# Two value projections in one pass over x, with x's first columns loaded ahead

## The chip, the core and the metric

The kernel runs on one core of a Trainium2 chip. A core has engines that work side by side, each through its own queue of instructions in order: TensorE (PE in the profile, with PEld for loading the stationary operand), VectorE (DVE), ScalarE (ACT), GpSimd (POOL) and SyncE (SP), which here only issues transfers. An instruction waits for semaphores that other engines or transfers raise, and everything behind it on its engine waits too. ScalarE can also issue transfers. The time is device microseconds of one execution, the median over several; lower is better.

## The reference, cut to what matters

The kernel is an encoder trunk of two layers over 256 tokens of width 1024. Each layer begins with an RMSNorm and one input projection, whose columns feed pooling, queries, keys, values and gates:

```python
def _token_mixer(xn, w_in, ...):
    u, q, k, v, g_pool, g_attn = jnp.split(xn @ w_in, SPLITS, axis=-1)
    ...
def reference(x, w_in, ..., norm1, ...):
    h = x
    for layer in range(DEPTH):
        h = h + _token_mixer(_rmsnorm(h, norm1[layer]), w_in[layer], ...)
        h = h + _conv_ffn(_rmsnorm(h, norm2[layer]), w_up[layer], ...)
    return _rmsnorm(h, norm_f)
```

The values v have 3 x 512 columns, one set of 512 for each head group. The change concerns the first two sets (g = 0 and g = 1) of layer 0, with which the kernel begins. Since RMSNorm multiplies row t of x by one number r(t) and column k by a gain, v = r(t) * sum over k of x(t,k) * (gain(k) * w(k,c)): the kernel starts on plain x with weights scaled by the gains, and multiplies by r(t) when it evicts the sums.

## The kernel before

Every operand of a product is split into two parts, a high part h (a cast to the fp32r type) and a low part l (the rest), and a product of 128 channels is three matmuls of 128x512: high by high, low by high, high by low ("hh", "lh", "hl"). The class Weights holds the plan of all weight loads and splits: rows adds a load of w rows, use puts its pieces in line, load and load_by issue its transfers (load_by in parts, on SyncE), open_next makes a piece's split: ScalarE writes the high part (with the gain as scale, line 195; without, line 187), VectorE the low part (lines 196 and 188). The tiles are called raw (as loaded, three buffers), wh and wl (split, five buffers), or take an idle tile of another stage (m2, ybig, at2, k1).

x stands as h, 128 partitions by two tokens t by 1024 columns. The two "halves" t = 0, 1 of the 256 tokens are the rows of the sums. To be the stationary operand, x is turned: turn_x transposes 128-column blocks on TensorE into a PSUM tile xt_ps (line 706), ScalarE casts it to xuh, VectorE subtracts to xul (lines 709, 710).

begin (line 328) issues the first transfers: the gains on ScalarE's queue, then on SyncE x's columns 0 to 511 of both tokens between the first four weight quarters of 256 KB, then columns 512 to 1023. It warms TensorE with products of ones (line 363) and turns the gains into gcol. begin_values_of_x (line 688) is written out by hand, its order kept as it is: it sums the set g = 0 over the eight 128-channel chunks k (line 753), with squares of x on ScalarE and VectorE and the plain turned x (f0, f1) added up from its two parts by VectorE (whole, line 736). Then first_values (line 808), whose order a scheduler sets, makes r_ps (the row factors turned, line 816), multiplies f by gains and row factors and splits it into x2 (lines 820 to 826), the normalised x of all later products, and sums the set g = 1 on the kept xuh and xul in a second pass (line 838). keep_values (line 853) evicts the sums.

Behind this stage TensorE transposes parameters (prm_ps, line 378) and begins the projections of u from x2 (by_rows, rows_ps, line 635). Between them stand three products f_ps of the bias tables (build_bias, line 411), which need rr: VectorE makes it (lines 397, 398) from a small table, rb, loaded after prm_ps.

Of the kernel before, what the change touches and what calls it, by code (L numbers as in the profile page):

```python
# [10 lines left out]
F32 = mybir.dt.float32  # L11
# [5 lines left out]
P = 128  # L17
# [69 lines left out]
class Weights:  # L87
# [42 lines left out]
    def load_by(self, n):  # L130

        src, shape, tag = self.loads[self.n_loaded]
        t = self.pool.tile([P, *shape], F32, tag="raw", bufs=self.RAW, name=f"raw{self.n_loaded}")
# [32 lines left out]
    def open_next(self):  # L166
# [24 lines left out]
        def scaled(j):  # L191
            k = (i * shape[0] + j) % KD
# [25 lines left out]
def encoder(ctx, tc, x, w_in, w_pool, pool_scale, w_a, w_b, w_o, norm1, norm2, w_up, conv_w,  # L218
# [29 lines left out]
    for l in range(DEPTH):  # L248
        for g in range(2):
            c0 = C_V + g * 512  # L250
            slots = (("m2", 0, 2), ("m2", 1, 2), ("ybig",), ("at2",)) if g == 0 else ()
            for j in range(l > 0 and g == 0, 2):
                tag = "k1" if l == 0 and g == 1 and j == 0 else None
                W.use(rows(w_in[l], j * 512, 4, c0, 512, tag), slots[2 * j : 2 * j + 2])
        if l == 0:
            W.n_scaled = len(W.pieces)

# [70 lines left out]
    def begin():  # L328
# [4 lines left out]
        first, second = W.load_by(4), W.load_by(2)  # L333

        def part_of_x(t, n):
            nc.sync.dma_start(out=h[:, t, HALVES[n]], in_=xv[:, t, HALVES[n]])
# [12 lines left out]
        nc.vector.memset(ones, 1.0)  # L349
        make_identity(nc, ident)  # L350
# [6 lines left out]
        warm(ps, ones, WARM[1])  # L357
        return lambda n: warm(ps, ones, n)
# [329 lines left out]
    def begin_values_of_x():  # L688


        more = begin()
# [9 lines left out]
        def turn_x(t, c0, n=4):  # L701

            ks = slice(c0, c0 + n)
            pt = mmp.tile([P, n, P], F32, tag="mm", name="xt_ps")
            for k in range(n):
                nc.tensor.transpose(pt[:, k, :], h[:, t, (c0 + k) * P : (c0 + k + 1) * P], ident)

            def keep():
                nc.scalar.copy(out=xuh[:, ks, t, :], in_=pt)
                nc.vector.tensor_sub(out=xul[:, ks, t, :], in0=pt, in1=xuh[:, ks, t, :].bitcast(F32))  # L710

            return keep

        def square(t, n):
            cc = HALVES[n]
            junk = sm.tile([P, 512], F32, tag="s", name="junk")
            if n == 0:
                nc.scalar.activation(
                    junk, h[:, t, cc], AF.Square, scale=D**-0.5, accum_out=ss[t][:, n : n + 1]
                )  # L720
            else:
                nc.vector.scalar_tensor_tensor(
                    out=junk, in0=h[:, t, cc], scalar=1.0 / D, in1=h[:, t, cc],
                    op0=ALU.mult, op1=ALU.mult, accum_out=ss[t][:, n : n + 1],
                )
# [6 lines left out]
        def whole(n, tag):  # L732

            ks = slice(4 * n, 4 * n + 4)
            f = big.tile([P, 4, 2, P], F32, tag=tag, name="xu")
            nc.vector.tensor_add(out=f, in0=xuh[:, ks].bitcast(F32), in1=xul[:, ks].bitcast(F32))
            return f

        ps = [v_tile() for _ in range(2)]
        chunks, pieces = {}, []  # L740

        def split(k):
            if k % 2 == 0:
                pieces.append(W.n_split)
                chunks[k], chunks[k + 1] = W.open_next()
            return chunks[k]

        def product(t, k, kind):
            wh, wl = W.split[pieces[k // 2]]
            a, w = {"hh": (xuh, wh), "lh": (xul, wh), "hl": (xuh, wl)}[kind]  # L750
            first = k == 0 and kind == "hh"
            last = k == KD - 1 and kind == ("lh" if t else "hl")
            return nc.tensor.matmul(ps[t], a[:, k, t, :], w[:, k % 2, :], start=first, stop=last)  # L753

        def both(k):

            hi, lo = split(k)
            hi()
            return lo()

        def products(*steps):
            for t, k, kinds in steps:
                for kind in kinds:
                    last = product(t, k, kind)
            return last

        keep = turn_x(0, 0, 2), turn_x(0, 2, 2)
        keep[0]()
        both(0)
        keep += (turn_x(1, 0),)  # L770
        keep[1]()
        products((0, 0, ("hh", "lh")))
        keep[2]()
        products((0, 0, ("hl",)))
        both(1)
        products((1, 0, ("hh", "hl", "lh")), *((t, 1, ("hh", "lh", "hl")) for t in range(2)))
        both(2)
        products(*((t, 2, ("hh", "lh", "hl")) for t in range(2)))
        keep = turn_x(0, 4)
        both(3)  # L780
        square(0, 0)
        square(1, 0)
        square(0, 1)
        f0 = whole(0, "q0")
        keep()
        products((0, 3, ("hh", "lh", "hl")))
        keep = turn_x(1, 4)
        both(4)
# [667 lines left out]
```

## Time and profile before

| | us |
|---|---|
| median of 3 runs | 859.83 (858.93 to 860.11) |
| profiled execution | 858.9 |
| its span | 857.1 |
| PE busy in it | 849.9 |

The span is what the profile shows between the first and the last instruction. A line of a timeline gives start and length in us, the engine, the line of the kernel, the operation, "out<-in", the shapes, how many equal ones stand together, and in brackets the idle time ahead of it with what ended it. Durations of matmuls overlap, since they are pipelined: the distance of two starts says more than a length. The windows view gives, for a stretch, the busy time of each engine (PE, PEld, DVE, ACT, POOL, each with the number of instructions), the granted clock, the busy share of the transfer engines, and GB/s.

### The profile page before, as it was taken

The page shows a single profiled execution, that of the slowest core. Times are in us where ns is not written, and L with a number is a line of the kernel's source. Part 1 is how long each engine was busy: PE and PEld are TensorE (multiplying, and loading weights), DVE is VectorE, ACT ScalarE, POOL GpSimd, SP SyncE. Part 2 cuts the span into 40 slices and gives each one's busy share as a digit, 9 for nine tenths or more (in the row PEclk, how much of TensorE's full clock was granted, in tenths as well). Part 3 has the DMA queues.
Part 4 walks back from the last instruction along what each step waited for, and adds up shares of the span by engine and source line. Part 5 has one row for each costly group of instructions (what it writes and reads, how often), then busy time and mean ns, then how long its engine had stood idle before and what let it go on. Part 6 is the DMA issues. An engine that isn't in the chain of part 4 may idle for free.

```text
span 857.1 us, 11247 instructions
## 1 busy us (share of the span) xinstructions
PE 849.9 (99%) x4036; PEld 713.1 (83%) x4036; DVE 648.9 (76%) x914; ACT 476.6 (56%) x691; POOL 20.6 (2%) x53
## 2 busy tenths in 40 slices
PE   9999999999999999999999999999999999999997
PEld 7888888888888888888888889888888888888886
DVE  7967988566757798899556598886567657998874
ACT  7645565444635576767444446654445436766762
POOL 2110000000010000000000000000000000000001
PEclk9999999999999999999999999999999999999999
DMA  9687674764846777777526766747658266777751
GB/s 334 224 251 249 200 255 160 222 229 131 307 152 225 231 243 238 252 246 259 197 99 211 230 227 207 233 152 248 203 199 285 102 216 208 243 241 243 242 195 50
DMA packets 99260, 185.02 MB, mean 216 GB/s; under 512 B 9518, under 2 KB 26110, under 8 KB 99204
## 3 DMA queue, kind: packets, MB, share of 16 engines
q1 hardware_dynamic: 98692, 182.96, 64.3%
q0 software_dynamic: 496, 1.33, 0.6%
q8 instruction: 32, 0.52, 0.2%
q14 instruction: 24, 0.20, 0.1%
q10 hardware_dynamic: 16, 0.00, 0.0%
HBM read 160.12 MB, written 1.07 MB: 188 GB/s over the span
## 4 chain that ended last, share of the span: by engine, by line
PE 99%; ACT 0%; POOLq 0%; DVE 0%; issue 0%; POOL 0%; ACTq 0%
PE rows_ps L635 61%; PE res_ps L551 6%; PE res_ps L549 6%; PE res_ps L550 6%; PE v_ps L635 5%; PE proj_ps L521 3%; PE proj_ps L523 2%; PE v_ps L753 1%; PE v_ps L838 1%; PE s_ps L1020 1%; PE o_ps L1095 1%; PE s_ps L1015 1%; PE o_ps L1091 1%; PE xt_ps L482 1%; PE pool_ps L515 0%; PE pool_ps L514 0%
## 5 line engine op out<-in xcount | busy, mean ns | idle before, releaser
L188 DVE TENSOR_TENSOR wl<-raw,wh 128x1024 fp32r<-128x1024 f32 x278 | 336.8, 1217 | 148.5 <-ACT wh L187 144.7
L635 PE MATMUL rows_ps<-wh,x 128*128 128x512 f32 x1344 | 419.9, 390 | 0.0
L187 ACT CAST wh<-raw 128x1024 fp32r<-128x1024 f32 x278 | 289.4, 1049 | 215.9 <-PE rows_ps L635 129.2
L635 PEld LDWEIGHTS rows_ps<-wh,x 128*128 128x128 f32 x1344 | 252.3, 188 | 51.9
L635 PE MATMUL rows_ps<-wl,x 128*128 128x512 f32 x672 | 261.4, 389 | 0.0
L635 PEld LDWEIGHTS rows_ps<-wl,x 128*128 128x128 f32 x672 | 126.2, 188 | 25.9
L549 PE MATMUL res_ps<-wh,actq 128*128 128x512 f32 (+1 forms) x152 | 57.5, 378 | 0.0
L550 PE MATMUL res_ps<-wl,actq 128*128 128x512 f32 (+1 forms) x152 | 57.4, 378 | 0.0
L551 PE MATMUL res_ps<-wh,actk 128*128 128x512 f32 (+1 forms) x152 | 57.4, 378 | 0.0
L635 PE MATMUL rows_ps<-wh,po 128*128 128x512 f32 x128 | 41.2, 393 | 0.0
L550 PEld LDWEIGHTS res_ps<-wl,actq 128*128 128x128 f32 x152 | 28.6, 188 | 5.4
L549 PEld LDWEIGHTS res_ps<-wh,actq 128*128 128x128 f32 x152 | 28.6, 188 | 5.4
L551 PEld LDWEIGHTS res_ps<-wh,actk 128*128 128x128 f32 x152 | 28.6, 188 | 5.3
L521 PE MATMUL proj_ps<-x,wh 128*128 128x512 f32 x128 | 32.2, 393 | 0.0
L670 DVE STREAM_TRANSPOSE up_rows<-rows_ps 128x512 f32<-128x512 f32 x40 | 26.2, 692 | 3.1 <-PE rows_ps L635 3.1
L635 PEld LDWEIGHTS rows_ps<-wh,po 128*128 128x128 f32 x128 | 24.0, 188 | 5.0
L448 ACT ACTIVATE junk<-h 128x512 f32<-128x512 f32 (+1 forms) x20 | 10.9, 547 | 30.8 <-DVE h L446 30.8
L1323 ACT ACTIVATE yg<-a,prm 128x256 f32<-128x256 f32 x44 | 26.5, 602 | 1.5
L549 PE MATMUL res_ps<-wh,m 128*128 128x512 f32 (+1 forms) x72 | 26.9, 374 | 0.0
L521 PEld LDWEIGHTS proj_ps<-x,wh 128*128 128x128 f32 x128 | 23.1, 189 | 4.2
L550 PE MATMUL res_ps<-wl,m 128*128 128x512 f32 (+1 forms) x72 | 26.4, 366 | 0.0
L551 PE MATMUL res_ps<-wh,m 128*128 128x512 f32 (+1 forms) x72 | 26.3, 366 | 0.0
(213 smaller groups left out, 1046.5 us busy)
## 6 DMA issues: line engine op xcount, KB each, us to landing
raw<-in_w_in_dram SPq DMA_DIRECT2D x58, 1024.0 KB, 5.6
raw<-in_w_up_dram SPq DMA_DIRECT2D x40, 1024.0 KB, 5.6
raw<-in_w_down_dram SPq DMA_DIRECT2D x22, 1024.0 KB, 5.2
up_turned<-up_rows SPq DMA_DIRECT2D x160, 64.0 KB, 4.2
raw<-in_w_a_dram SPq DMA_DIRECT2D x8, 1024.0 KB, 4.8
raw<-in_w_o_dram SPq DMA_DIRECT2D x8, 1024.0 KB
qk<-qk_rows SPq DMA_DIRECT2D x64, 64.0 KB, 2.7
pt<-rows SPq DMA_DIRECT2D x64, 64.0 KB, 4.9
```

What stands on the lines that cost most here:

```text
L187: lambda: nc.scalar.copy(out=h, in_=src),
L188: lambda: nc.vector.tensor_sub(out=l, in0=src, in1=h.bitcast(F32)),
L448: nc.scalar.activation(junk[:, 0 : cc.stop - cc.start], h[:, t, cc], AF.Square, scale=D**-0.5, accum_out=ss[:, n : n + 1],)
L482: nc.tensor.transpose(pt[:, k, :], xn[:, c0 : c0 + P], ident)
L521: nc.tensor.matmul(ps, wh(k), x2[:, k], start=(k == 0), stop=False)
L523: nc.tensor.matmul(ps[:, 1], wl(k), x2[:, k, 0], start=False, stop=(k == nk - 1))
L549: nc.tensor.matmul(ps, ah, wh, start=first, stop=False)
L550: nc.tensor.matmul(ps, ah, wl, start=False, stop=False)
L551: nc.tensor.matmul(ps, al, wh, start=False, stop=last)
L635: nc.tensor.matmul(ps, x2[:, 2 * n + j, part, t, :], w[:, j, :], start=(n + m == 0), stop=(n == of - 1 and m == 5),)
L670: nc.vector.transpose(out=out[:, :, t].rearrange("p j c r -> p c j r"), in_=ps[t].rearrange("p (c j r) -> p c j r", c=4, j=4),)
L1323: nc.scalar.activation(y, aj, AF.Identity, bias=b, scale=w1)
```

## The change

Both value sets are summed in one pass: for each chunk k of x there are now twelve products, two sets by two tokens by three kinds, into four PSUM tiles held together. The weights are put in line in the order of that pass, the two sets' pieces in turn. begin loads only columns 0 to 255 of x ahead, the first token's by SyncE, the second's by ScalarE's queue; then two quarters of each set's weights; then columns 256 to 1023 of both tokens; then the rest of the weights. The first part of xuh is cast by VectorE. ScalarE writes plain turned x straight from PSUM (copy) and makes all four squares; the sums whole on VectorE are gone. An instruction of one column on ScalarE ("table") stands ahead of its first real one, which moves the load of its function table there. The normalised x2 is made within the pass, by hand (normalised), with the first two unscaled weight pieces between (ahead), and the evictions come once, at the end. The bias tables start one visit later.

```diff
-        first, second = W.load_by(4), W.load_by(2)
...
-        part_of_x(0, 0)
-        next(first)
-        part_of_x(1, 0)
-        for _ in range(3):
-            next(first)
-        part_of_x(0, 1)
-        part_of_x(1, 1)
-        for _ in range(2):
-            next(second)
-        W.load(4)
+        for t, queue in enumerate((nc.sync, nc.scalar)):
+            queue.dma_start(out=h[:, t, 0:256], in_=xv[:, t, 0:256])
+        loads = [W.load_by(n) for n in (4, 4, 2, 2)]
+        for n in (0, 1, 0, 1):
+            next(loads[n])
+        for t in range(2):
+            nc.sync.dma_start(out=h[:, t, 256:], in_=xv[:, t, 256:])
+        for n in (0, 1, 0, 1, 2, 3, 2, 3):
+            next(loads[n])
         ones = sm.tile([P, P], F32, tag="s", name="ones")
         nc.vector.memset(ones, 1.0)
+        nc.scalar.copy(out=sm.tile([P, 1], F32, tag="rz", name="table"), in_=ones[:, 0:1])
...
+        def products(k, g):
+            for t in range(2):
+                for kind in ("hh", "lh", "hl"):
+                    last = product(k, g, t, kind)
             return last
...
+        rest = keep0(nc.vector.tensor_copy)
+        low = split(0, 0)
+        rest()
+        rest = keep1()
+        low()
...
+        both(0, 1)
+        copy0(fs[0])
+        both(1, 0)
+        copy1(fs[0])
+        products(0, 1)
+        both(1, 1)
+        turns = turn_x(0, 2, 2), turn_x(1, 2, 2)
+        products(1, 0)
+        square(0, 0)
+        square(0, 1)
+        for t, (keep, copy) in enumerate(turns):
+            rest = keep()
+            copy(fs[0])
+            rest()
+            both(2, t)
+        square(1, 0)
+        pool = square(1, 1)
+        products(1, 1)
+        turns = [turn_x(t, 4) for t in range(2)]
+        for g in range(2):
+            products(2, g)
+            both(3, g)
+        for t, (keep, copy) in enumerate(turns):
+            rest = keep()
+            copy(fs[1])
+            rest()
+            both(4, t)
+            products(3, t)
...
+        for t in range(2):
+            for g in range(2):
+                keep_values(t, g, ps[g][t], rs)
+        W.behind = (pool, last)
         return x2
...
-            if l == 0:
+            if l == 0 and count > 1:
                 next(bias, None)
```

What this does to the engines' queues, at three places. First TensorE, from the transposition of the gains to its second set of transposes of x (m is the tile m2, which holds both parts of set 0's first weights; wh and wl are the parts of set 1's). Before:

```order
L354 MATMUL gain_ps<-ident,grows 128x8
L363 MATMUL warm_ps<-ones 128x128
L706 MATMUL xt_ps<-ident,h 128x128 x8
L753 MATMUL v_ps<-m_139,xuh 128x512
...
L706 MATMUL xt_ps<-ident,h 128x128 x4
L753 MATMUL v_ps<-m_139,xuh 128x512
```

With the change:

```order
L358 MATMUL gain_ps<-ident,grows 128x8
L708 MATMUL xt_ps<-ident,h 128x128 x4
L366 MATMUL warm_ps<-ones 128x128
L754 MATMUL v_ps<-m_149,xuh 128x512
...
L754 MATMUL v_ps<-wl_162,xuh 128x512
L708 MATMUL xt_ps<-ident,h 128x128 x4
L754 MATMUL v_ps<-m_149,xuh 128x512
```

The left-out rows are products: 17 more before, 10 more with the change (with those shown six of set 0, then six of set 1, all of chunk 0). Four transposes instead of eight stand ahead of the first product, and the second set of transposes has come from behind 18 products to behind 12.

Second, SyncE from its first transfer to the end of x. Before:

```order
L336 DMA h<-in_x_dram 128x512
L138 DMA raw_91<-in_w_in_dram 128x512
L336 DMA h<-in_x_dram 128x512
L138 DMA raw_91<-in_w_in_dram 128x512 x3
L336 DMA h<-in_x_dram 128x512 x2
```

With the change:

```order
L343 DMA h<-in_x_dram 128x256
L142 DMA raw_92<-in_w_in_dram 128x512
L142 DMA raw_94<-in_w_in_dram 128x512
L142 DMA raw_92<-in_w_in_dram 128x512
L142 DMA raw_94<-in_w_in_dram 128x512
L348 DMA h<-in_x_dram 128x768 x2
L142 DMA raw_92<-in_w_in_dram 128x512
```

raw_92 is of set 0, raw_94 of set 1. Four weight quarters and all of x are issued first in both; the part of x that comes last is now three quarters of it, and ScalarE's queue takes one transfer of 128x256 that is not in these rows.

Third, VectorE around the end of the stage, up to the second step of rr. Before:

```order
L826 TENSOR_TENSOR x_276<-xu,x_276 128x2x256 x2
L863 SCALAR_TENSOR_TENSOR vl<-v_ps,rstd,vh 128x512 x2
L379 COPY prm<-prm_ps 128x96 x2
L380 TENSOR_SCALAR hps<-prm 128x8
L188 TENSOR_TENSOR wl_403<-raw_207,wh_402 128x1024
...
L188 TENSOR_TENSOR wl_411<-raw_249,wh_410 128x1024
L397 CAST rr<-rb 128x128
L188 TENSOR_TENSOR wl_434<-raw_300,wh_433 128x1024
L398 TENSOR_TENSOR rr<-rb,rr 32x128
```

With the change:

```order
L382 COPY prm<-prm_ps 128x96 x2
L383 TENSOR_SCALAR hps<-prm 128x8
L775 TENSOR_TENSOR x_134<-xu,x_134 128x2x256
L885 SCALAR_TENSOR_TENSOR vl<-v_ps,rstd,vh 128x512
...
L192 TENSOR_TENSOR wl_418<-raw_274,wh_417 128x1024
L885 SCALAR_TENSOR_TENSOR vl<-v_ps,rstd,vh 128x512
L192 TENSOR_TENSOR wl_422<-raw_274,wh_421 128x1024
L400 CAST rr<-rb 128x128
L192 TENSOR_TENSOR wl_440<-raw_321,wh_439 128x1024
L401 TENSOR_TENSOR rr<-rb,rr 32x128
```

One of the last two subtractions of x2 and both evictions vl have moved behind the copy of prm, and three splits instead of four stand between prm and the second step of rr.

More of the change, by code (lines that the diff above doesn't have):

```diff
@@ L767, in begin_values_of_x @@
[L767 to L782, printed above, removed]
@@ L798, in begin_values_of_x @@
[L798 to L818 removed]
+        x2 = two_parts("x", "x2")
@@ L825, in first_values @@
             nc.scalar.copy(out=oh, in_=f)
[L826 to L843 removed]
+            return lambda: nc.vector.tensor_sub(out=ol, in0=f, in1=oh.bitcast(F32))
@@ new lines, in values_of_x, with ahead @@
+        lows = [split(7, g) for g in range(2)]
+        def ahead():
+            (hi, lo), = W.open_next()
+            hi()
+            return lo
+        rest = normalised(0, rows, fs[0])
+        for low in lows:
+            last = low()
+        for g in range(2):
+            products(5, g)
+        W.load(7)
+        W.n_got = W.n_split
+        for piece in pieces.values():
+            W.free(piece)
+        low = ahead()
+        more = normalised(2, rows, fs[0])
+        rest()
+        low()
```

184 lines of the change are left out of this document (80 added, 104 removed).

## Prediction

> **What bounds the kernel now.** I read the page first: busy time by engine and the chain of work that ended last. The span is TensorE's own work (PE busy 849.9 of 857.1 us, the chain 99% PE), so a change counts only by the moment at which TensorE passes from the stage that it rewrites into work that is the same in both kernels.
>
> ```profile
> span 857.1 us, 11247 instructions
> PE 849.9 (99%) x4036; PEld 713.1 (83%) x4036; DVE 648.9 (76%) x914; ACT 476.6 (56%) x691; POOL 20.6 (2%) x53
> PE 99%; ACT 0%; POOLq 0%; DVE 0%; issue 0%; POOL 0%; ACTq 0%
> ```
>
> Then the timeline of PE over that stage. Columns: start, length, engine, line, operation, count.
>
> ```profile
> 1.04 2.50 PE L363 MATMUL gain_ps<-ones 128*128 128x128 f32 x10 [1.04 <-DVE mhalf L351]
> ...
> 6.11 0.78 PE L753 MATMUL v_ps<-m,xuh 128*128 128x512 f32 x1
> ...
> 9.37 0.62 PE L753 MATMUL v_ps<-m,xuh 128*128 128x512 f32 x2
> ...
> 10.96 0.60 PE L706 MATMUL xt_ps<-ident,h 128*128 128x128 f32 x4
> 11.31 0.48 PE L753 MATMUL v_ps<-m,xuh 128*128 128x512 f32 x1
> 11.63 0.40 PE L753 MATMUL v_ps<-m,xul 128*128 128x512 f32 x1
> ...
> 18.98 0.38 PE L816 MATMUL r_ps<-ident,rstd 128*128 128x128 f32 x2
> 19.12 0.48 PE L838 MATMUL v_ps<-wh,xuh 128*128 128x512 f32 x1
> ...
> 29.87 0.39 PE L838 MATMUL v_ps<-wh,xul 128*128 128x512 f32 x1
> 30.10 0.33 PE L378 MATMUL prm_ps<-ident,prow 96*128 96x96 f32 x2
> 30.21 0.48 PE L635 MATMUL rows_ps<-wh,x 128*128 128x512 f32 x1
> ...
> 37.56 0.61 PE L411 MATMUL f_ps<-onehot_r,rr 128*128 128x512 f32 x2
> ```
>
> The reader is to see three things. The common work begins at 30.21, with the first rows_ps. The 48 products of line 838 start from 19.12 to 29.87, 47 steps, so one product costs 0.229 us when nothing waits. And the first twelve products start from 6.11 to 9.37, some 3.5 us with the last one's own step (the row at 9.37 holds the twelfth and the thirteenth), where twelve unhindered ones take 2.75.
>
> Both kernels do 96 such products, 22.0 us. From 6.11 to 30.21 are 24.1 us, less 22.0, less two groups of four transposes (10.96 to 11.31 and a longer step of 0.32 behind it, so 0.44 each, 0.9) and 0.2 for r_ps and prm_ps: 1.0 us of waiting is left. That, and a start before 6.11, is all that can be won.
>
> **When the transfers land.** The stage lives on loads, so I asked for the data moved since the start (last column GB/s), and for the instructions that waited for a landing.
>
> ```profile
> 0.00:4.50 4.50, 3.46 (x15) 3.21 (x16) 0.34 (x3) 1.28 (x1) 0.69 (x6) 1.00 0.54 180
> 0.00:7.20 7.20, 6.12 (x24) 5.14 (x25) 1.94 (x7) 3.25 (x6) 0.69 (x6) 1.00 0.67 218
> 0.00:8.70 8.70, 7.62 (x30) 6.02 (x31) 3.44 (x9) 4.36 (x7) 0.69 (x6) 1.00 0.73 243
> ```
> ```profile
> 5.33 0.72 PEld L706 LDWEIGHTS xt_ps<-ident,h 128*128 128x128 f32 x4 [0.41 <-issue]
> ```
> ```profile
> 9.15 0.72 ACT L195 ACTIVATE m<-raw,gcol 128x512 fp32r<-128x512 f32 x1 [0.84 <-DMA raw<-in_w_in_dram]
> 9.78 0.61 ACT L718 ACTIVATE junk<-h 128x512 f32<-128x512 f32 x1
> 10.30 0.19 ACT L718 ACTIVATION_READ_ACCUMULATOR junk<-h 128x1 f32 x1
> 10.39 0.62 ACT L718 ACTIVATE junk<-h 128x512 f32<-128x512 f32 x1
> ```
>
> ```profile
> h<-in_x_dram SPq DMA_DIRECT2D x4, 256.0 KB, 3.6
> raw<-in_w_in_dram SPq DMA_DIRECT2D x4, 256.0 KB
> ```
>
> Every early transfer is 256 KB, 262,000 bytes. The transposes of the third in line (x's second token, first half) began at 5.33, after an idle stretch; 786 KB had been moved by about 4.4 (180 GB/s times 4.5 us is 810 KB). So use follows the moving by 0.9 us. ScalarE waited for the sixth in line (the fourth quarter of the weights) until 9.15; 1,573 KB had been moved by 7.2 (218 times 7.2 is 1,570), so that one came 1.95 us behind. By 8.7 us 2,114 KB had been moved.
>
> **The change, part by part.**
>
> *x in another order.* SyncE now issues 128 KB of x, four quarters of weights (two of each set), and then the other 768 columns of x, two transfers of 393 KB; ScalarE's queue adds the second token's first 128 KB. Ahead of and including the last of x stand again four weight quarters and all of x, 2,097 KB. That amount was moved by 8.65 us, so x's rest can be used between 9.55 (0.9 behind) and 10.6 (1.95 behind). I take 10.6: the sixth in line is the nearest row to a transfer that ends eighth.
>
> *Transposes of columns 256 to 511 after twelve products.* Before, the second set of transposes stood behind 18 products, at 10.96, and found its x there. Now twelve products (two weight chunks by two tokens by three) need only the early 256 columns, and then TensorE's queue holds four transposes that need x's rest; products of the next chunk stand behind them, though their weights are there. The first product moves forward: today the cast of x and then the scaled weights are made on ScalarE in turn.
>
> ```profile
> 4.94 0.37 ACT L709 CAST xuh<-xt_ps 128x256 fp32r<-128x256 f32 x1 [2.31 <-PE xt_ps L706]
> 5.21 0.72 ACT L195 ACTIVATE m<-raw,gcol 128x512 fp32r<-128x512 f32 x1
> ```
> ```profile
> 3.79 0.17 DVE L355 COPY gcol<-gain_ps 128x8 f32<-128x8 f32 x1 [2.79 <-PE gain_ps L354]
> ```
>
> The scaled weights can start from 3.96 (gains copied) to 5.21 (as today, where they did not wait for their load), so the first product starts between 4.9 and 6.1; I take 5.4. Twelve products at today's 3.5 us end at 8.9. From there to 10.6 TensorE waits, 1.7 us (0 to 2.2 over the two ranges). So the earlier start is worth nothing: it only lengthens the wait.
>
> *The rest of the pass.* From the landing at 10.6: 0.4 to get two transposes done, 84 products by 0.229 (19.2), eight more transposes (0.9), r_ps and prm_ps with their steps (0.3): 31.4 against 30.21, **+1.2 us** (+0.1 with landings at 9.55).
>
> *ScalarE writes plain x and all squares.* Two wide sums on VectorE go; ScalarE gains four 256-wide copies (0.37), two 512-wide ones (0.59), and two squares (0.61), and loses one cast, 3.5 us. I count nothing. Its queue from x's rest on (two squares, two casts, two copies, two scaled chunks, two squares, two scaled chunks, a wide cast, a wide copy, the chunk for k=4) is about 7.7 us by the distances of the starts above (0.27 a narrow cast, 0.61 a square, 0.63 a chunk, 0.5 a wide cast), from 9.5, when the first token's rest lands, to 17.2; TensorE needs that chunk after 36 more products, near 20. The cover is 2.8 us.
>
> *Other edits at nothing.* The table load is earlier but was over before 4.94; SyncE's further issues lie beside TensorE's work; the hold on four weight pieces that goes (queue_behind) concerned pieces that TensorE reads only from the first rows_ps on.
>
> *Normalised x and the bias tables.* The stage's last casts now sit close to its end. VectorE must finish rr before f_ps, which stands 7.35 us behind the first rows_ps in both orders.
>
> ```profile
> 29.04 1.29 DVE L826 TENSOR_TENSOR x<-xu,x 128x512 fp32r<-128x512 f32 x2
> 30.25 1.40 DVE L863 SCALAR_TENSOR_TENSOR vl<-v_ps,rstd,vh 128x512 fp32r<-128x512 f32 x2
> 31.57 0.41 DVE L379 COPY prm<-prm_ps 128x96 f32<-128x96 f32 x2
> ...
> 31.97 1.22 DVE L188 TENSOR_TENSOR wl<-raw,wh 128x1024 fp32r<-128x1024 f32 x1
> ...
> 36.83 0.28 DVE L398 TENSOR_TENSOR rr<-rb,rr 32x128 fp32r<-32x128 f32 x1
> ```
> ```profile
> 29.43 1.05 ACT L187 CAST wh<-raw 128x1024 fp32r<-128x1024 f32 x1
> ```
>
> Today rr ends at 37.11, 6.9 us behind rows_ps and 0.45 ahead of f_ps. After: ScalarE's cast of the fifth weight piece needs a buffer that TensorE gives up with the stage's last product, and the last cast of x is queued behind it: 1.05 plus 0.6, so VectorE's last subtraction of x begins about 1.8 us behind rows_ps. Behind that stand 0.65 (x), twice 0.7 (vl), three times 1.15 (wl), rr and its rest 0.45: 5.9 us, so rr is ready at 7.7. f_ps waits **0.35 us**; 0 if VectorE is a little ahead, 0.9 if ScalarE's evictions come late.
>
> Sum: 1.2 + 0.35, **+1.55 us**. The profiled run took 858.9 us (span 857.1 and 1.8 around it), 0.9 under the median of 859.83; the forecast on the median is 859.83 + 1.55 = **861.4 us**, 0.18%. About 0.2% (1.7 us) is what a measurement of this kernel can tell from no change, so this forecast lies just inside.
>
> **Rivals.** *No wait for x.* If x's rest lands by 8.9 (0.25 us behind its moving), the stage ends at 8.9 + 0.44 + 19.2 + 1.2 = 29.75, or 29.2 with a first product at 4.9, −0.5 to −1.0 us: 858.8 to 859.6. For it: the load before 5.33 was used 0.9 behind. Against it: even that is too late, and at 9.15 it was 1.95. Even this is not faster by 0.2%.
>
> *The clock falls in the gap (slower).* TensorE starts slow: four transposes are loaded in 0.87 us at 4.05, while four at 10.96 are through in 0.35.
>
> ```profile
> 4.05 0.87 PEld L706 LDWEIGHTS xt_ps<-ident,h 128*128 128x128 f32 x4
> ```
>
> The slow spell held from 1.04 to past 6.0 (the loads at 5.33 are as slow), some 5.5 us, of which about half was lost. If the gap of 1.7 us sends TensorE back there, the price is 2.8 us for a spell as long, 864.2, and 862.8 for one of half its length. It decides if the gap, broken only by two transposes, counts as idle. [...] No gap of that length stands in this trace.
>
> *A late supply.* If ScalarE's queue slips by more than its 2.8 us of cover (x later than 11.5, say), the loss grows with it: 862.5 to 864.
>
> *The early columns do not come early.* Two queues may share what one had; the first product then stays near 6.1, twelve products end at 9.6, and the end is the same 861.4, since x's rest decides.
>
> **How the numbers follow.** The wait for x of 0.1 to 1.25 us of loss, with f_ps, 58% (a third of it over 1.7 us once f_ps and the runs' spread of 0.6 us are added); no wait 18%, a fifth of which the spread may carry under −1.7; clock 13%; late supply 11%. So slower by over 0.2%: 0.19 + 0.13 + 0.10, 0.42; faster by over 0.2%: 0.04; within: 0.54. The range runs from the no-wait case, 858.8, to the middle of the clock's, 863.5.
>
> **What would show it.** Right: PE idle before the transposes of line 708 that follow the first twelve products, until 9.5 to 10.7, ended by a DMA; then no idle of 0.2 us until f_ps (line 414), and that one ended by VectorE's rr (line 401); the first product near 5.4; the first rows_ps near 31.4. Wrong: transposes of line 708 without idle (no wait), products twice 0.229 apart behind the gap (clock), or PE waiting for line 199 on ScalarE past k=3 (supply).

## The result, and the profile after

The changed kernel took 860.28 us (median of 22 runs, 859.33 to 861.16); the kernel before, over 22 runs now, 858.72 (858.52 to 860.30). The ratio is 1.0015, with a 95% interval of 1.0009 to 1.0021: slower by 0.15%, inside the 0.2% that the prediction named as its limit. Of the 22 runs of the kernel before, sixteen lie at 858.52 to 859.01 us and six at 859.68 to 860.30; its profile belongs to the sixteen, and why the six are longer stays open, since no trace of them was kept. The profiled execution of the changed kernel took 860.27. Its page, first the span, then busy time by engine, then the chain that ended last by engine:

```profile
span 858.5 us, 11269 instructions
PE 849.0 (99%) x4036; PEld 712.2 (83%) x4036; DVE 645.9 (75%) x910; ACT 477.7 (56%) x702; POOL 18.5 (2%) x53
PE 98%; DMA 1%; SPq 0%; ACT 0%; issue 0%; POOLq 0%; DVE 0%; POOL 0%; ACTq 0%
```

TensorE is still all of it, but the chain, which held no transfer before, now has 1% of DMA. PE's timeline of the changed kernel shows where that lies:

```profile
3.68 0.69 PE L708 MATMUL xt_ps<-ident,h 128*128 128x128 f32 x2
4.99 0.44 PE L708 MATMUL xt_ps<-ident,h 128*128 128x128 f32 x2 [0.63 <-DMA h<-in_x_dram]
5.27 0.39 PE L366 MATMUL warm_ps<-ones 128*128 128x128 f32 x2
5.63 0.50 PE L754 MATMUL v_ps<-m,xuh 128*128 128x512 f32 x1
...
8.38 0.40 PE L754 MATMUL v_ps<-wl,xuh 128*128 128x512 f32 x1
9.49 0.41 PE L708 MATMUL xt_ps<-ident,h 128*128 128x128 f32 x2 [0.71 <-DMA h<-in_x_dram]
10.49 0.41 PE L708 MATMUL xt_ps<-ident,h 128*128 128x128 f32 x2 [0.59 <-DMA h<-in_x_dram]
10.66 0.47 PE L754 MATMUL v_ps<-m,xuh 128*128 128x512 f32 x1
10.97 0.39 PE L754 MATMUL v_ps<-m,xul 128*128 128x512 f32 x1
11.20 0.63 PE L754 MATMUL v_ps<-m,xuh 128*128 128x512 f32 x2
...
31.08 0.48 PE L638 MATMUL rows_ps<-wh,x 128*128 128x512 f32 x1
...
38.21 0.39 PE L638 MATMUL rows_ps<-wl,x 128*128 128x512 f32 x1
38.66 0.47 PE L414 MATMUL f_ps<-onehot_r,rr 128*128 128x512 f32 x1
```

Three stretches matter. The second token's early columns arrive late, so TensorE stands idle ahead of 4.99. The twelve products run from 5.63 to 8.38, and TensorE then waits for x's rest twice, for the first token until 9.49 and for the second until 10.49. The first rows_ps starts at 31.08 against 30.21, **0.87 us later**; f_ps starts 7.58 us behind it instead of 7.35, **0.23 more**. TensorE's last matmul starts 1.08 us later (851.79 against 850.72), so nothing else is lost up to there.

The other 0.27 us of the span's 1.35 lies at the very end, behind the issue of the last output transfer (855.05 against 853.97). There SyncE waits for the semaphores of the transfers in a fixed order, and in the trace one wait follows the other by 0.06 us when nothing is left to wait for. In the kernel before the two output transfers have the last two places of nine. With the change they have the fourth and the fifth, so four more waits, 0.24 us, stand behind the last landing. Every trace of this document fits: from that issue to the end of the span pass 3.15 us with no wait behind the output's (the kernel before, and f4 below), 3.27 to 3.28 with two (e2, e10, f2, f5), and 3.40 to 3.43 with four (the changed kernel and the rest).

The wait at f_ps fits the predicted cause; its row names no releaser, and e4 below tests it. VectorE's timeline, at the last cast of x and at rr:

```profile
32.58 0.69 DVE L775 TENSOR_TENSOR x<-xu,x 128x512 fp32r<-128x512 f32 x1 [0.56 <-ACT x L774]
...
38.23 0.28 DVE L401 TENSOR_TENSOR rr<-rb,rr 32x128 fp32r<-32x128 f32 x1
```

VectorE waits for ScalarE's cast of x (line 774), and rr ends at 38.51, just past the 38.43 (31.08 + 7.35) at which f_ps would have begun.

### The profile page after: what moved, and what is told of

It reads as the page before. It is cut to its first block, busy times and chain, and to the rows that moved or that the text cites. A ratio compares the mean times of both kernels' runs of the same rounds, so it can differ in the third digit from the quotient of the medians.

```text
span 858.5 us, 11269 instructions
## 1 busy us (share of the span) xinstructions
PE 849.0 (99%) x4036; PEld 712.2 (83%) x4036; DVE 645.9 (75%) x910; ACT 477.7 (56%) x702; POOL 18.5 (2%) x53
## 4 chain that ended last, share of the span: by engine, by line
PE 98%; DMA 1%; SPq 0%; ACT 0%; issue 0%; POOLq 0%; DVE 0%; POOL 0%; ACTq 0%
PE rows_ps L638 61%; PE res_ps L552 6%; PE res_ps L553 6%; PE res_ps L554 6%; PE v_ps L638 5%; PE proj_ps L524 3%; PE v_ps L754 2%; PE proj_ps L526 2%; PE s_ps L1041 1%; PE o_ps L1116 1%; DMA h<-in_x_dram 1%; PE s_ps L1036 1%; PE o_ps L1112 1%; PE xt_ps L485 1%; PE pool_ps L518 0%; PE pool_ps L517 0%
## 5 line engine op out<-in xcount | busy, mean ns | idle before, releaser
L451 ACT ACTIVATE junk<-h 128x512 f32<-128x512 f32 (+1 forms) x20 | 10.9, 547 | 30.9 <-DVE h L449 30.8
```

Source lines behind the costliest of these rows:

```text
L451: nc.scalar.activation(junk[:, 0 : cc.stop - cc.start], h[:, t, cc], AF.Square, scale=D**-0.5, accum_out=ss[:, n : n + 1],)
```

## The experiments

The theory was the prediction's: the wait for x's rest costs about 1 us, the late rr a quarter of one. The rivals were ScalarE's added work, the second queue, and a later x. Ratios are against the kernel before, run beside each kernel: its median was 858.93 us beside e1, e2, e4 and e10, and 859.16 beside e3, e5 and e7. One execution of each kernel was traced.

**e1 (e1_turn_later): the second set of transposes behind 24 products instead of 12**, past the landing of x's rest.

```diff
-        turns = turn_x(0, 2, 2), turn_x(1, 2, 2)
         products(1, 0)
+        products(1, 1)
+        turns = turn_x(0, 2, 2), turn_x(1, 2, 2)
         square(0, 0)
...
-        products(1, 1)
         turns = [turn_x(t, 4) for t in range(2)]
```

> TensorE transposes columns 256 to 511 of x behind 24 products instead of 12; transfers as in the changed kernel. Theory (the loss is TensorE's wait for x's rest, 1.9 us of idle in two pieces before 10.66, and 0.23 before f_ps): no wait for a transfer is left, since 24 products end near 11.2 and x's rest landed by 10.4; a wait of some 0.7 us for ScalarE's cast and VectorE's rest of the newly turned columns takes its place, so the first rows_ps comes near 29.9 instead of 31.08 and the time falls by 1.1 us, to the kernel before or 0.1 us under it. Rival (ScalarE's added copies and squares bound the pass): the first rows_ps stays within 0.3 us of 31.1 and ScalarE, not a transfer, ends TensorE's waits from there on.

Measured: 861.46 us, ratio 1.0024 (1.0015 to 1.0032). The wait for x is gone, and still the first rows_ps is at 32.15, later than the changed kernel's 31.08. PE's timeline of e1:

```profile
5.36 0.69 PE L708 MATMUL xt_ps<-ident,h 128*128 128x128 f32 x2 [0.99 <-DMA h<-in_x_dram]
5.84 0.64 PE L366 MATMUL warm_ps<-ones 128*128 128x128 f32 x2
6.13 0.77 PE L754 MATMUL v_ps<-m,xuh 128*128 128x512 f32 x1
6.70 0.63 PE L754 MATMUL v_ps<-m,xul 128*128 128x512 f32 x1
7.13 1.48 PE L754 MATMUL v_ps<-m,xuh 128*128 128x512 f32 x3
8.41 0.58 PE L754 MATMUL v_ps<-m,xul 128*128 128x512 f32 x1
8.82 0.40 PE L754 MATMUL v_ps<-wh,xuh 128*128 128x512 f32 x1
9.06 0.40 PE L754 MATMUL v_ps<-wh,xul 128*128 128x512 f32 x1
...
14.71 0.50 PE L754 MATMUL v_ps<-m,xuh 128*128 128x512 f32 x1 [0.26 <-ACT m L199]
```

Two things took the gain. The products stand 0.43 us apart (three from 7.13 to 8.41) until 8.8, and only then 0.23. And the casts behind the transposes, with the next weights, come on ScalarE after them: a wait of 0.26 us at 14.71. A miss; the first of the two was in no theory yet.

**e2 (e2_rest_split): columns 256 to 511 in transfers of their own, ahead of the other 512.**

```diff
-            nc.sync.dma_start(out=h[:, t, 256:], in_=xv[:, t, 256:])
+            nc.sync.dma_start(out=h[:, t, 256:512], in_=xv[:, t, 256:512])
+        for t in range(2):
+            nc.sync.dma_start(out=h[:, t, 512:], in_=xv[:, t, 512:])
```

> x's rest comes in two pieces per token, columns 256 to 511 of both tokens first, then 512 to 1023; TensorE's order as in the changed kernel. Theory: the awaited part ends after 1,573 KB instead of 2,097 KB and lands 1.0 to 1.3 us earlier, near 9.2; the gap before the product that follows it shrinks from 1.9 to about 0.8 us, the first rows_ps comes near 30.0, the time falls by 1.0 us. Rival (ScalarE bounds the pass): first rows_ps within 0.3 us of 31.1. Rival (smaller transfers land later because each carries its own ending): the awaited part lands less than 0.5 us earlier.

Measured: 859.88 us, ratio 1.0009 (1.0000 to 1.0018). No wait for x, but the products are 0.43 us apart until 10.1, the twelve end only near 10.9, and the first rows_ps is at 31.65. Less than half of the expected gain is there in the median.

**e4 (e4_bias_later): the bias tables one visit later still.**

```diff
-            if l == 0 and count > 1:
+            if l == 0 and count > 2:
```

> The bias tables start one visit later still, so f_ps stands twelve products later; all else as in the changed kernel. Theory: the wait before f_ps (0.23 us) goes, nothing takes its place, first rows_ps unchanged near 31.1; the time falls by 0.2 us, within what five rounds can tell. Rival (f_ps waits for the onehot cast of ScalarE or the table's transfers, and what follows the tables is late instead): a new wait of 0.2 us or more before the scores that read the tables.

Measured: 859.91 us, ratio 1.0011 (1.0002 to 1.0019). In its profile the wait at f_ps is gone: TensorE is 1.53 us late at the first rows_ps and 1.47 at its last matmul. The step is confirmed; its 0.23 us cannot be told from the changed kernel by times. The first rows_ps is at 31.75, not near 31.1 as expected. PE's timeline of e4 shows that its twelve products took 5.18 us:

```profile
5.81 0.77 PE L754 MATMUL v_ps<-m,xuh 128*128 128x512 f32 x1
...
10.65 0.51 PE L754 MATMUL v_ps<-wl,xuh 128*128 128x512 f32 x1
10.99 0.60 PE L708 MATMUL xt_ps<-ident,h 128*128 128x128 f32 x4
```

**e10 (e10_all): e2 and e4 together, and the second set of transposes behind 18 products.** Its diff is e2's and e4's, and this:

```diff
-        turns = turn_x(0, 2, 2), turn_x(1, 2, 2)
         products(1, 0)
+        turns = turn_x(0, 2, 2), turn_x(1, 2, 2)
```

> x's rest in two pieces per token as in the run before, the transposes of columns 256 to 511 behind 18 products, and the bias tables one visit later. Theory: no TensorE wait over 0.2 us between the first product and f_ps; first rows_ps near 29.5, f_ps without its wait of 0.23 us; 1.7 us under the changed kernel and 0.5 to 0.7 us under the kernel before. Rival (the one pass has another bound): not under the kernel before.

Measured: 859.38 us, ratio 1.0004 (0.9995 to 1.0013). Behind the first product no row names a wait, yet the first rows_ps is at 30.74, 1.2 us behind the expectation: products are 0.43 us apart until 8.5. The median is 0.9 us under the changed kernel's, not 1.7; three of the eleven runs (858.18 to 858.54) are as low as expected.

**e3 (e3_one_queue): both early parts of x on SyncE's queue.**

```diff
-        for t, queue in enumerate((nc.sync, nc.scalar)):
+        for t, queue in enumerate((nc.sync, nc.sync)):
```

> Both early parts of x are issued by SyncE, none by ScalarE's queue. Theory (x's rest decides the end of the stage, what comes before it only fills the wait): the second token's early part lands within 0.5 us of its 4.95, and whether the first product comes before or after 5.63, the first rows_ps stays within 0.4 us of 31.1 and the time within 0.4 us. Rival (the late landing of ScalarE's transfer costs the time): the first product comes 0.4 us or more earlier and the time falls by as much.

Measured: 862.32 us, ratio 1.0032 (1.0022 to 1.0042). PE's timeline of e3:

```profile
3.68 1.11 PE L708 MATMUL xt_ps<-ident,h 128*128 128x128 f32 x4
...
5.71 0.80 PE L754 MATMUL v_ps<-m,xuh 128*128 128x512 f32 x1 [0.48 <-ACT m L199]
...
10.14 0.57 PE L754 MATMUL v_ps<-wh,xul 128*128 128x512 f32 x1
10.55 0.39 PE L754 MATMUL v_ps<-wl,xuh 128*128 128x512 f32 x1
10.78 0.38 PE L708 MATMUL xt_ps<-ident,h 128*128 128x128 f32 x2
11.39 0.41 PE L708 MATMUL xt_ps<-ident,h 128*128 128x128 f32 x2 [0.23 <-DMA h<-in_x_dram]
```

All four transposes now run without a gap. The idle stretch has only moved behind them, to the first weights (5.71), the products are slow until 10.5, and x's second token lands 0.9 us later than with the change (11.39 against 10.49). The time rose by 2.0 us, which neither expectation had. On the second queue x's early columns do land later (4.95 us with the change, 3.95 here), but that costs nothing: here the first weights, which land at 4.84, hold the first product just as late, and x's rest is later. The trace explains only part of the rise. It is of one of the four runs at 860.84 to 861.10; the other five, the median among them, lie at 862.32 to 862.71 with a mean granted clock of 0.996 to 0.997 against 0.998 to 0.999, and why stays open.

**e5 (e5_plain_dve): plain x written by VectorE again.**

```diff
-                nc.scalar.copy(out=f[:, c0 % 4 : c0 % 4 + n, t, :], in_=pt)
+                nc.vector.tensor_copy(out=f[:, c0 % 4 : c0 % 4 + n, t, :], in_=pt)
```

> The plain turned x is copied by VectorE instead of ScalarE; all else as in the changed kernel. Theory (ScalarE's added work is covered): first rows_ps within 0.2 us of 31.1, time unchanged within 0.3 us. Rival (ScalarE bounds the pass): first rows_ps earlier by up to 1.5 us, the sum of the six copies being 2.1 us of ScalarE's time.

Measured: 860.74 us, ratio 1.0012 (1.0003 to 1.0021), not to be told from the change; first rows_ps at 31.91 (31.1 expected), products slow until 11.0. From the product behind the second transposes to the first rows_ps pass 20.42 us here (11.49 to 31.91) and in the changed kernel (10.66 to 31.08), so ScalarE's added copies do not bound.

**e7 (e7_rest_later): x's rest behind six weight quarters instead of four.**

```diff
-        for n in (0, 1, 0, 1):
+        for n in (0, 1, 0, 1, 0, 1):
...
-        for n in (0, 1, 0, 1, 2, 3, 2, 3):
+        for n in (0, 1, 2, 3, 2, 3):
```

> x's rest is issued behind two more weight quarters, so that 524 KB more stand ahead of it. Theory: TensorE's gap grows one for one with the landing, by 1.3 us (524 KB at about 400 GB/s) to some 3.2 us in all, first rows_ps near 32.4, time 1.3 us up; products behind the gap stay 0.229 us apart. Rival (a gap of this length costs TensorE its clock): products behind it stand up to 0.46 us apart for up to 5.5 us, and the time rises by 2.5 to 4 us.

Measured: 860.68 us, ratio 1.0015 (1.0005 to 1.0024): the same as the change. The expected loss is absent, and PE's timeline shows why:

```profile
5.13 0.69 PE L708 MATMUL xt_ps<-ident,h 128*128 128x128 f32 x2 [0.77 <-DMA h<-in_x_dram]
...
9.03 0.63 PE L754 MATMUL v_ps<-wh,xul 128*128 128x512 f32 x1
9.46 0.61 PE L754 MATMUL v_ps<-wl,xuh 128*128 128x512 f32 x1
...
10.62 0.85 PE L708 MATMUL xt_ps<-ident,h 128*128 128x128 f32 x4
```

Slow products keep TensorE busy until 10.6; the wait that a later x would lengthen is hardly there.

### A second theory: TensorE's late full rate

In seven of these profiles the products stand 0.43 us apart from the first one up to some moment between 8.5 and 11.0 us, and 0.23 apart behind it; in the kernel before that moment is at 6.81, behind its first two products, and in the changed kernel at 4.38, ahead of the first. The granted clock in the view by windows reads 1.00 all the while (so in the rows that the prediction shows from 0.00 on), so the distance between starts tells it, and that column does not: the record of the clock begins with this moment, and the view counts what lies ahead of it as full. The table gives the idle time that the rows show ahead of the second token's transposes or of the first product, that moment (the trace's record of the clock gives it, and the distances agree), the first rows_ps, and the medians. The first nine rows were there when the theory was made.

| kernel | idle ahead, us | full rate from | first rows_ps | median | lowest to highest (runs) |
|---|---|---|---|---|---|
| before | 0.04 | 6.81 | 30.21 | 858.72 | 858.52 to 860.30 (22) |
| after | 0.63 | 4.38 | 31.08 | 860.28 | 859.33 to 861.16 (22) |
| e1 | 0.99 | 8.81 | 32.15 | 861.46 | 859.42 to 861.90 (11) |
| e2 | 1.10 | 10.14 | 31.65 | 859.88 | 858.27 to 861.05 (11) |
| e10 | 0.74 | 8.53 | 30.74 | 859.38 | 858.18 to 860.38 (11) |
| e4 | 0.68 | 10.88 | 31.75 | 859.91 | 859.58 to 860.64 (11) |
| e3 | 0.48 | 10.51 | 31.95 | 862.32 | 860.84 to 862.71 (9) |
| e5 | 0.82 | 11.02 | 31.91 | 860.74 | 859.86 to 861.11 (10) |
| e7 | 0.77 | 9.93 | 31.62 | 860.68 | 860.28 to 861.09 (10) |
| f1 (after, filled) | none | 6.31 | 30.49 | 859.86 | 859.56 to 860.61 (11) |
| f2 (e10, filled) | none | 5.97 | 29.76 | 858.23 | 858.05 to 859.15 (11) |
| f3 (e1, filled) | none | 4.97 | 30.67 | 859.78 | 859.22 to 860.84 (11) |
| f4 (before, less warming) | 0.59 + 0.75 | 9.75 | 31.38 | 860.49 | 858.84 to 861.79 (11) |
| f5 (f2, start ahead) | none | 4.98 | 29.43 | 858.42 | 858.06 to 858.92 (11) |

The theory: the idle stretch ahead of 5 us delays full rate, and a late full rate and the wait for x's rest lie one on the other, so that taking away either alone shows the other. No run shows the bounds of 6.9, 7.9 and 10.3 us that the expectations below set for full rate; the filled kernels had it from 4.97 to 6.31 us, f4 from 9.75. Five kernels test the theory; beside them the kernel before took 858.86 us (f1 to f4) and 858.80 (f5). "Filled" is this edit; wait() issues one product of ones (two rows of the trace), whose result is not used:

```diff
-        (keep0, copy0), (keep1, copy1) = turn_x(0, 0, 2), turn_x(1, 0, 2)
-        wait()
+        keep0, copy0 = turn_x(0, 0, 2)
+        for _ in range(3):
+            wait()
+        keep1, copy1 = turn_x(1, 0, 2)
+        wait()
```

**f1 (f1_warm): the changed kernel, filled.**

> The changed kernel with three more products of ones on TensorE between the first token's two transposes and the second token's, where it now stands idle from about 3.95 to 5.0-5.5 us. They compute nothing that is used. [...] With the stretch filled, full rate begins between 4.4 and 7.9 us in every execution, the twelve first products end near 8.9, and the wait for x's rest (until about 10.5) is there every time: first rows_ps at 31.0 to 31.3, time 859.9 to 860.3, with less spread from run to run, no gain in the mean. Rival A (idle time has nothing to do with it, full rate comes after a fixed time or by chance): full rate as scattered as before, in most profiles past 8.5, no wait for x. Rival B (x's second token is what sets the start): the start of the first product stays at 5.6 to 6.2, and nothing else changes.

Measured: 859.86 us, ratio 1.0009 (1.0001 to 1.0018). PE's timeline of f1:

```profile
4.16 1.49 PE L366 MATMUL warm_ps<-ones 128*128 128x128 f32 x6
5.44 0.63 PE L708 MATMUL xt_ps<-ident,h 128*128 128x128 f32 x2
5.87 0.60 PE L366 MATMUL warm_ps<-ones 128*128 128x128 f32 x2
6.15 0.55 PE L754 MATMUL v_ps<-m,xuh 128*128 128x512 f32 x1
6.54 0.40 PE L754 MATMUL v_ps<-m,xul 128*128 128x512 f32 x1
...
9.09 0.38 PE L708 MATMUL xt_ps<-ident,h 128*128 128x128 f32 x2
9.93 0.41 PE L708 MATMUL xt_ps<-ident,h 128*128 128x128 f32 x2 [0.46 <-DMA h<-in_x_dram]
```

From the second product on they stand 0.23 us apart, and the wait for x is back, as the theory says. It is smaller than expected (0.46; x's second token at 9.93 instead of 10.49), so the first rows_ps is at 30.49 and not past 31, and the time is just under the expected range. The runs lie within 1.05 us (11 runs) instead of 1.83 (22). Rival A's late rate did not show, nor does it in f2, f3 and f5 below; in Rival B the first product did stay at 6.15, but the rest of its sentence failed.

**f2 (f2_all_warm): e10, filled.**

> The kernel of e10_all (columns 256 to 511 in a transfer of their own, second set of transposes behind 18 products, bias tables a visit later) with the same three products of ones in the idle stretch. Theory (two costs, late full rate and the wait for x's rest, lie one on the other, and here both are taken away): full rate by 7.9 us, no wait for x, the first rows_ps at 29.5 to 30.0 against 30.21 in the kernel before and 30.74 in e10_all, no wait at f_ps, time 0.2 to 0.7 us under the kernel before (858.2 to 858.7). Rival (full rate does not depend on the idle stretch): first rows_ps as in e10_all, 30.5 to 31.2, time 0.3 to 0.6 us over the kernel before. Rival (something else, ScalarE's or VectorE's chain, sets the pass once TensorE is fast): full rate early, yet idle stretches behind k=1 that a ScalarE or VectorE line ends, and the first rows_ps past 30.2.

Measured: 858.23 us, ratio 0.9993 (0.9984 to 1.0002); first rows_ps at 29.76, no wait for x, full rate from 5.97. All three numbers are in the theory's ranges. Against f1, which has the early rate too but keeps the waits for x's rest and at f_ps, TensorE's last matmul starts 1.02 us earlier (850.20 against 851.22): with the rate out of the way, that is about what the two waits cost. Its profiled span is 856.7 us against 857.1.

**f3 (f3_later_warm): e1, filled.**

> The kernel of e1_turn_later (second set of transposes behind 24 products) with the same three products of ones in the idle stretch. Theory (the order gained nothing there because the late full rate had already eaten the wait): with full rate by 7.9 us the 24 products end near 11.4 to 11.9, behind the landing of x's rest, so no wait for x; the first rows_ps falls from 32.15 to 30.1-30.7, with some 0.5 us of it a wait for the casts and scaled weights behind the transposes; f_ps may wait up to 0.5 more. Time 859.2 to 859.9 against 861.46 in e1_turn_later. Rival (moving the transposes starves ScalarE and VectorE, which then supply the next chunk late): full rate early, but the first rows_ps stays at 31.3 or later with a wait of 1 us or more behind the transposes; time 860.5 or more.

Measured: 859.78 us, ratio 1.0012 (1.0003 to 1.0020), against e1's 1.0024 (1.0015 to 1.0032); first rows_ps at 30.67 instead of 32.15. PE's timeline:

```profile
11.50 1.47 PE L708 MATMUL xt_ps<-ident,h 128*128 128x128 f32 x12
13.24 0.50 PE L754 MATMUL v_ps<-m,xuh 128*128 128x512 f32 x1 [0.26 <-ACT m L199]
```

Of the 1.5 us, 0.3 are an earlier first product (5.83 against 6.13) and the rest the earlier full rate; the wait for ScalarE behind twelve transposes is the same 0.26 as in e1. So the rival here holds too, at a small size: the late transposes do starve the next chunk a little.

**f4 (f4_before_cold): the kernel before, with one product of ones instead of five at the start.**

```diff
-WARM = (5, 1)
+WARM = (1, 1)
```

> The kernel before with one product of ones instead of five ahead of the gains' transposition; nothing else. TensorE then is idle from about 1.6 to 3.4 us, before any product. Theory (an idle stretch at the start delays full rate): full rate begins between 6.9 and 10.3 us instead of up to 7.9 (6.81 in the profile before), each product before it costs 0.2 us more, so the first rows_ps moves from 30.21 to 30.5-31.9, and the time rises by 0.5 to 1.5 us. Rival (full rate is not tied to idle time): first rows_ps at 30.2, time unchanged within 0.2 us.

Measured: 860.49 us, ratio 1.0012 (1.0003 to 1.0020), and runs from 858.84 to 861.79. PE's timeline:

```profile
3.81 1.11 PE L706 MATMUL xt_ps<-ident,h 128*128 128x128 f32 x4 [0.59 <-DMA h<-in_x_dram]
5.67 1.09 PE L706 MATMUL xt_ps<-ident,h 128*128 128x128 f32 x4 [0.75 <-DMA h<-in_x_dram]
6.41 0.78 PE L753 MATMUL v_ps<-m,xuh 128*128 128x512 f32 x1
...
8.69 0.63 PE L753 MATMUL v_ps<-m,xul 128*128 128x512 f32 x1
9.11 0.63 PE L753 MATMUL v_ps<-m,xuh 128*128 128x512 f32 x1
9.54 0.49 PE L753 MATMUL v_ps<-m,xul 128*128 128x512 f32 x1
9.87 0.63 PE L753 MATMUL v_ps<-m,xuh 128*128 128x512 f32 x2
```

The idle time came in three pieces: 0.41 us ahead of the gains' transposition and the two that the rows show. Nothing of the change is in this kernel, and the same slow products appear until 9.75, with the first rows_ps at 31.38. Less work at the start costs 1.2 us there, 0.3 of it by the later first product (6.41 against 6.11) and the rest by products at 0.43; by the medians it is 1.6, a little over what was expected, by the ratio 1.0.

**f5 (f5_all_warm_ahead): f2 without the product of ones behind the second token's transposes.**

```diff
         keep1, copy1 = turn_x(1, 0, 2)
-        wait()
```

> The kernel of f2_all_warm without the product of ones behind the second token's transposes, so that the first product of the stage can start 0.4 us earlier (5.65 instead of 6.06); it also repeats that kernel's comparison in all else. Theory (with full rate early and the wait for x's rest gone, TensorE's start is what counts, and every part of an earlier start is kept): first product at 5.6 to 5.75, no wait for x (18 products end at 9.9 to 10.2), first rows_ps 29.4 to 29.6 against 29.76, time 0.6 to 1.1 us under the kernel before. Rival (the products behind the first are held by the supply of scaled weights and low parts): the first product is earlier, but the second token's stand idle, the first rows_ps stays near 29.76, time 0.3 to 0.7 under the kernel before. Rival (x's first half lands too late): idle ahead of the transposes behind 18 products, ended by a transfer, with the gain lost there.

Measured: 858.42 us against 858.80, ratio 0.9992 (0.9983 to 1.0001). PE's timeline:

```profile
5.69 0.50 PE L756 MATMUL v_ps<-m,xuh 128*128 128x512 f32 x1
...
9.80 0.40 PE L756 MATMUL v_ps<-m,xuh 128*128 128x512 f32 x1
10.03 0.60 PE L710 MATMUL xt_ps<-ident,h 128*128 128x128 f32 x4
10.39 0.48 PE L756 MATMUL v_ps<-wh,xuh 128*128 128x512 f32 x1
```

Eighteen products run without a wait and the four transposes find their x. The first rows_ps is at 29.43, as expected, 0.78 us ahead of the kernel before, and the span is 856.4 against 857.1. By the median the gain is 0.4 us, less than the 0.6 to 1.1 expected, by the ratio 0.7. The intervals of f2 and f5 each just reach 1, so neither is shown to beat the kernel before; both lie under the changed kernel's interval.

## Why the prediction was right, point by point

**The sum.** Forecast +1.55 us, measured +1.56 between the medians of 22 runs, or 1.3 by the ratio. That the two agree so closely is partly luck. In the profiled pair the two terms came to 1.08 us instead of 1.55, and 0.27 came from the waits at the end of the program, a term that the prediction does not have. The forecast of 861.4 was put on a median of three runs, two of which (859.83 and 860.11) are among the six high ones of 22; that median lay 1.1 us above the one of 22, and the forecast is 1.1 us too high by it.

**The wait for x's rest.** Right: x was taken as usable from 10.6 and the last of it came at 10.49 (2,097 KB were moved by about 8.8 us instead of 8.65, and the last transfer landed at 10.36, 1.6 behind instead of 1.95); the twelve products were to end at 8.9 and ended at 8.6 (the start at 8.38 and one step). Only the transposes were priced too high: the first token's were already done when the second's could start, and 0.17 us instead of 0.4 stood behind the landing. So +0.87 instead of +1.2.

**rr and f_ps.** Right in cause; VectorE's last subtraction of x began 1.50 us behind rows_ps (1.8 forecast), so rr came 7.43 behind it (7.7 forecast), and the wait was 0.23 instead of 0.35. e4 removes it.

**ScalarE's added work at nothing.** Right: its chunk for k=4 began at 16.36 and ended at 17.11 (17.2 forecast), with no wait of TensorE for it, and e5 moves nothing.

**The early columns.** The first product came at 5.63 (5.4 forecast). But the second token's columns, on ScalarE's queue, landed 3.6 us after their issue (1.34 to 4.95), the first token's on SyncE's after 2.6 (0.73 to 3.31); and in the other kernels with this order the first product came at 5.8 to 6.2. In e3 one queue does no better (5.71).

**"So the earlier start is worth nothing."** This step failed as a general statement, though not in the profiled run. What was worth nothing here was an earlier start ahead of a wait; what stood ahead of the start decided the rate. The sum priced twelve products "at today's 3.5 us". That figure carries the kernel before's own moment of full rate, 6.81, which stretches its first step to 0.57 us, and later steps of 0.39 and 0.34 where TensorE waited for VectorE; in the profiled run of the change the twelve took 2.98. The change opened an idle stretch ahead of 5 us, and in seven kernels that keep one the moment came at 8.5 to 11.0, where twelve products take up to 5.2 us (5.81 to 10.99 in e4). That this hardly shows in the result is because the two costs overlap: in e4, e5 and e7 the first rows_ps is 0.5 to 0.8 us later than in the profiled run of the change, not by the 2.2 us that such twelve products take longer. These three traces are of runs at the upper end of their kernels' spread (860.64, 861.11 and 860.91).

Only one of the changed kernel's 22 runs was traced. Of the nine traced kernels with such an idle stretch it alone has the early rate. By that count, an estimate, the traced run is the exception, and most of the other 21 had the late rate, hidden wholly or in part by the wait for x's rest; this is not shown. The eight runs with a mean granted clock of 0.999 took 860.42 to 861.16 us and the fourteen with 0.998, the traced one among them, 859.33 to 860.47. f1's median is 0.4 us lower with a narrower spread, but the two intervals overlap. So the wait for x's rest is shown as the cause in the traced run and, by f2, in f1; how the loss divides in the other runs stays open.

**The clock as a rival.** The rival put such a loss in the wrong place. It let the clock fall in the gap behind the twelve products; the profile after has products 0.23 us apart behind the gaps too (10.97 and 11.20), so idle stretches of 0.7 and 0.6 us took nothing of the rate. In the kernels that lose by the clock, it had not yet risen, and the cause was an idle stretch the prediction did not look at, 4 us earlier. The sign of a slow start was read from unlike rows (0.87 us is for four loads, 0.35 for four products; the four loads at 10.73 took 0.59), but it was right: full rate came at 6.81.

**The no-wait case.** It was priced at 0.2 to 1.0 us under the base, not faster by 0.2%. f2 and f5 are that case with the early rate, 0.6 and 0.4 us under theirs: priced about right. (Its upper time, 859.6, does not follow from its −0.5 us, which gives 859.3.)

## What to carry to other kernels

Where a kernel starts from loads, look at the distance of equal matmuls at its start before pricing anything there: a price from the first microseconds is valid only as long as the work ahead of it stays as dense (here twelve products took 2.98 us in one kernel and up to 5.2 in another). If a change opens an idle stretch on TensorE before full rate is reached, fill it with products that need no data (here full rate then came at 4.97 to 6.31 us, and at 8.5 to 11.0 in eight kernels with such a stretch), and compare only then what a new order of loads is worth. When removing the one wait that a profile names gains nothing, suspect a second cost beneath it, and take both away in one run.

## What the runs showed of the hardware

A 128x512 product took 0.43 us before a certain moment and 0.23 behind it. The traces' record of the clock gives that moment, which the table of the second theory lists, and the length of the stretch at full rate: 846.51 us in ten of the fourteen traces and 849.92 in the other four. Counted from TensorE's first work at 1.04 us, or from the end of its last idle stretch ahead of the rise, full rate came 3.34 us later (the changed kernel, 1.04 to 4.38) to 5.84 us later (e4, 5.04 to 10.88); the idle time between was 0.01 us in the changed kernel and 0.04 in the kernel before, and no row of the others names any. What sets the moment within these times was not shown. Behind the rise idle time did less: in the changed kernel the two waits for x's rest, 0.71 and 0.59 us, left the products 0.23 us apart (10.97 and 11.20).

Where TensorE was kept busy from its first work at 1.04 us, the rise came at 4.97 to 6.31 us in the four filled kernels and at 6.81 in the kernel before; with idle stretches of 0.48 to 1.10 us ahead of the first product it came at 8.5 to 11.0, in eight kernels of nine. In the ninth, the changed kernel, it came at 4.38, as the idle stretch of 0.63 us began; in seven of the eight that stretch began at 4.4 to 5.2 us and the rise had not come.

Runs spread more where the start is idle (11 runs each): over 2.5 us in e1 against 1.6 in f3, over 2.2 in e10 against 1.1 in f2.
